# Attention's second exponential written to SBUF, with two shared buffers in place of three

## The chip, the cores and the metric

The kernel runs on one core of one Trainium2 chip. The metric is device time in microseconds (us), lower is better. A core has five engines that matter here: TensorE (PE; its weight loads are listed apart as PEld), VectorE (DVE), ScalarE (ACT), GpSimd (POOL) and SyncE (SP, which issues most DMAs). Each works through its own instructions in order and waits for the others by semaphores. PSUM is the memory that PE writes; SBUF holds everything else on the chip.

## The reference

One layer of an encoder on 1024 prompt tokens and 64 tokens of a running stream. One input projection feeds eight heads of forgetting attention and four heads of a gated recurrence (HGRN2); both are gated and meet in an output projection. The change touches the attention of the prompt alone:

```python
def fox_attend(q, k, v, c_q, c_k, q_pos, k_pos):
    s = jnp.einsum('bqhd,bkhd->bhqk', q.astype(F32), k.astype(F32)) * (FOX_HEAD_DIM ** -0.5)
    s = s + (jnp.swapaxes(c_q, 1, 2)[..., :, None] - jnp.swapaxes(c_k, 1, 2)[..., None, :])
    mask = k_pos[None, :] <= q_pos[:, None]
    s = jnp.where(mask, s, -jnp.inf)
    p = jax.nn.softmax(s, axis=-1)
    return jnp.einsum('bhqk,bkhd->bqhd', p.astype(v.dtype), v)
```

`q` and `k` have 8 heads of 64 columns; `c` is the running sum of the log forget values.

## The kernel before

**Precision.** Matmuls run on a rounded float type (`F32R`). To keep float32 accuracy a value is split into a high part, rounded to `F32R`, and a low part, the rest; products of high with high, high with low and low with high are added up. For the attention weights the high part `ph` is the exponential of the scores written as `F32R` (L848). The exponential is then computed a second time in float32 (L849), and DVE subtracts `ph` from it to get the low part `pl` (L850).

**Stages.** A first part projects the values (to about 80 us). Then comes attention, in which PE also runs the projections of queries, keys and others as filler (L248, L229; `Filler` and `merge` hand them out by cost). Then the recurrence with the remaining projections, and at last the output projection.

**Attention.** The heads go in the order of `PAIRS`, two heads `s` to a pair `p_`. Each head has two chunks `c` of 512 queries, with 4 and 8 blocks `b` of 128 keys. The last four blocks of a chunk cross the diagonal and have 512, 384, 256 and 128 query columns. `scores` (L834) makes a block: two matmuls into a PSUM bank `st` (L842 and L843), the mask added by DVE on the diagonal (L845), the two exponentials on ACT, the subtraction on DVE. `values` (L856) multiplies with the values two blocks later (`LAG = 2`): three matmuls of line L867, with `ph`, `pl` and again `ph`, into a bank `av`. At the end of a chunk L873 to L875 divide by the row sums through a tile of the tag `tmp`. The sample's exponentials (`pt`, L898 to L900) and one step of the projection `hi` (L238) use the same tag.

**Buffers.** `st` has two banks (`PSB`), so a block's L842 needs that the block two before it has been read out. `ph` and `pl` have three buffers each (`PB`), `tmp` has three (`TMPB`).

**Work beside it.** While a head runs, `prepare` readies the next: ACT copies high parts (L717, L737, L748), POOL subtracts low parts (L722, L738, L754), PE and DVE find row maxima (L795, L797, L801, L812 to L814), DVE makes two columns of them (L760, L761) and SP brings them into rows of `QY` by small DMAs (L780). `QY` is read by L843 and L896. Weights come by DMA into one raw buffer (L163); ACT makes the high part in four pieces (L174), POOL the low part (L175), and the next load starts after the last piece.

**Order.** The order in which the generators hand out the work is the program's. A list scheduler then places each engine's instructions, so that a change of what a tile waits for also moves neighbours.

Of the kernel before, what the change touches and what calls it, by code (L numbers as in the profile page):

```python
# [8 lines left out]
F32 = mybir.dt.float32  # L9
F32R = mybir.dt.float32r  # L10
U8 = mybir.dt.uint8
AF = mybir.ActivationFunctionType
ALU = mybir.AluOpType
AX = mybir.AxisListType

P = 128
# [10 lines left out]
EPS = 1e-6  # L27
NEG = -3.0e38

WBUFS, PB, TMPB, NBUF, OGB, GB = 4, 3, 3, 8, 3, 7  # L30
PSB = dict(pj=2, tp=2, st=2, av=2)


# [30 lines left out]
def f32(ap):  # L64
    return ap.bitcast(F32)
# [3 lines left out]
def tile_fox_hgrn2(  # L69
# [7 lines left out]
    act, dve, pool, pe, sync = nc.scalar, nc.vector, nc.gpsimd, nc.tensor, nc.sync  # L77
# [7 lines left out]
    def nm(s):  # L85
        cnt[0] += 1
        return f"{s}_{cnt[0]}"
# [4 lines left out]
    def bank(tag):  # L92
        return ps.tile([P, 512], F32, tag=tag, name=nm(tag), bufs=PSB[tag])
# [561 lines left out]
    with actx:  # L655
        ap = actx.enter_context(tc.tile_pool(name="att", bufs=1, reuse_waits="tile"))
        a2 = actx.enter_context(tc.tile_pool(name="att2", bufs=2, reuse_waits="tile"))
# [176 lines left out]
        def scores(p_, s, c, b):  # L834

            kx, ky, qx, qy = KX[s], KY[s], QX[s], QY[s]
            q0 = max(0, b - 4 * c) * P
            n = 512 - q0
            ks = slice(b * P, (b + 1) * P)
            qs = slice(c * 512 + q0, (c + 1) * 512)  # L840
            st = bank("st")
            pe.matmul(st[:, :n], kx[:, ks], qx[:, qs], start=True, stop=False)  # L842
            pe.matmul(st[:, :n], ky[YM[s], ks], qy[YM[s], qs], start=False, stop=True)  # L843
            if b >= 4 * c:
                dve.tensor_tensor(st[:, :P], st[:, :P], kmask[:], op=ALU.add)  # L845
            ph = a2.tile([P, 512], F32R, tag="ph", name=nm("ph"), bufs=PB)
            pl = a2.tile([P, 512], F32R, tag="pl", name=nm("pl"), bufs=PB)
            act.activation(ph[:, :n], st[:, :n], AF.Exp)  # L848
            act.activation(st[:, :n], st[:, :n], AF.Exp)  # L849
            dve.tensor_tensor(pl[:, :n], st[:, :n], f32(ph[:, :n]), op=ALU.subtract)  # L850
            queue.append((p_, s, c, b, ph, pl))
            return 2 * n / 2.4

# [24 lines left out]
        def chunk_main(p_, s, c):  # L878
            for b in range(4 * (c + 1)):
                yield scores(p_, s, c, b)  # L880
                yield values() if len(queue) > LAG else 0.0
# [615 lines left out]
    for i, rows, src in tok_tiles[:SAMPLE_POS] + tok_tiles[NT:] + tok_tiles[SAMPLE_POS:NT]:  # L1497
# [11 lines left out]
        st = fin.tile([P, 1], F32, tag="sst", name=nm("sst"), bufs=3)  # L1509
# [94 lines left out]
```

## Time and profile before

| what | value |
|---|---|
| median of 3 runs | 689.65 us (689.0 to 690.16) |
| the profiled execution | 689.64 us, span 687.9 us |
| mean granted TensorE clock | 0.999 |
| share of PE, DVE, ACT, POOL in the span | 98%, 61%, 47%, 22% |
| L849 (second exponential), 96 times | 46.6 us on ACT |
| L850 (subtraction), 96 times | 53.0 us on DVE |
| L867 (three groups), 96 times each | 33.4, 33.0 and 32.4 us on PE |

The span goes from the first to the last instruction. A group's row in the profile reads: line, engine, operation, tiles written and read, shape, how often; then busy us and mean ns of one; then the idle time of the engine before them and what ended it. A row of a timeline begins with the start and the length in us; idle time before it, with what ended it, stands in brackets. A row of the waits reads: who waited for whom, us in total, times, longest. Matmuls overlap, and their ends are modelled, so that their lengths are longer than the spacing of their starts.

### The profile page before, as it was taken

To read this page: it belongs to the slowest core of one execution; us is meant where nothing else is said; L and a number is where in the kernel's file an instruction comes from. 1 tells how busy PE (TensorE), PEld (TensorE's weight loads), DVE (VectorE), ACT (ScalarE), POOL (GpSimd) and SP (SyncE) were. 2 spreads that over 40 slices of the span, in tenths; PEclk is the share of its full clock that TensorE was granted. 3 is DMA by queue.
4 is the path that set the end of the run, shared out by engine and by line. 5 is a ranking of instruction groups with operands and counts; after the bars stand their busy time and mean duration, and the time that the engine had idled before them with its cause. 6 is when DMAs were issued, how large, how long until landed. Compare 5 with 4: busy or idle time off the path is not lost.

```text
span 687.9 us, 13216 instructions
## 1 busy us (share of the span) xinstructions
PE 674.5 (98%) x4952; PEld 608.4 (88%) x4952; DVE 423.0 (61%) x1058; ACT 325.2 (47%) x826; POOL 152.2 (22%) x217
## 2 busy tenths in 40 slices
PE   9999999999999999899999999999999999999996
PEld 7888998898889899689999999999999998878885
DVE  4536267776666774775687365563965679754541
ACT  6845644746465664656443423432423344414532
POOL 4045832523343323301000100010000100103422
PEclk9999999999999999999999999999999999999999
DMA  8923312222222311211311110121111115421211
GB/s 314 338 84 112 109 40 80 65 61 45 65 55 52 71 26 40 80 12 32 116 43 32 43 33 31 32 71 35 32 40 54 40 37 184 126 83 61 93 47 61
DMA packets 40715, 51.17 MB, mean 74 GB/s; under 512 B 22870, under 2 KB 25766, under 8 KB 40652
## 3 DMA queue, kind: packets, MB, share of 16 engines
q1 hardware_dynamic: 40476, 50.25, 24.6%
q8 instruction: 39, 0.64, 0.4%
q14 instruction: 24, 0.20, 0.1%
q10 hardware_dynamic: 176, 0.09, 0.1%
HBM read 36.32 MB, written 9.56 MB: 67 GB/s over the span
## 4 chain that ended last, share of the span: by engine, by line
PE 67%; DVE 1%; DMA 1%; SPq 1%; POOL 1%; ACT 1%; issue 0%; POOLq 0%; DVEq 0%; ACTq 0%
PE pj L248 30%; PE pj L1383 13%; PE pj L229 7%; PE av L867 4%; PE st L842 2%; PE st L1114 1%; PE st L843 1%; PE st L1274 1%; PE pj L1377 1%; PE tp L795 1%; SPq L780 1%; DMA wr<-in_w_t_dram 1%; PE tp L1301 1%; PE av L1301 1%; PE tp L1303 1%; PE tp L1255 1%
## 5 line engine op out<-in xcount | busy, mean ns | idle before, releaser
L248 PE MATMUL pj<-hT,whi 128*128 128x364 f32 (+1 forms) x1152 | 218.8, 330 | 0.0
L248 PEld LDWEIGHTS pj<-hT,whi 128*128 128x128 f32 x1152 | 194.2, 188 | 6.6 <-issue 0.3
L248 PE MATMUL pj<-hT,wlo 128*128 128x364 f32 (+1 forms) x576 | 115.6, 332 | 0.0
L248 PEld LDWEIGHTS pj<-hT,wlo 128*128 128x128 f32 x576 | 96.9, 188 | 3.1 <-issue 0.2
L848 ACT ACTIVATE ph<-st 128x512 fp32r<-128x512 f32 (+1 forms) x96 | 46.8, 488 | 65.3 <-DVE st L845 42.7
L850 DVE TENSOR_TENSOR pl<-st,ph 128x512 fp32r<-128x512 f32 (+1 forms) x96 | 53.0, 553 | 30.7 <-ACT st L849 30.1
L109 POOL TENSOR_SCALAR rr<-ss 128x4 f32<-128x4 f32 (+1 forms) x12 | 2.3, 190 | 257.2 <-ACT og L1307 256.9
L1383 PE MATMUL pj<-hT,mx 128*128 128x512 f32 (+1 forms) x264 | 56.3, 374 | 0.0
L1383 PEld LDWEIGHTS pj<-hT,mx 128*128 128x128 f32 x264 | 46.2, 188 | 10.0
L175 POOL TENSOR_TENSOR wlo<-wr,whi 128x256 fp32r<-128x256 f32 (+1 forms) x52 | 36.8, 736 | 75.6 <-ACT ph L848 39.7
L174 ACT ACTIVATE whi<-wr 128x256 fp32r<-128x256 f32 (+1 forms) x112 | 38.1, 406 | 29.5 <-PE pj L248 18.1
L849 ACT ACTIVATE st<-st 128x512 f32<-128x512 f32 (+1 forms) x96 | 46.6, 485 | 0.0
L842 PE MATMUL st<-QX,KX 128*128 128x512 f32 (+1 forms) x96 | 34.9, 364 | 2.7 <-DVE pl L850 2.2
L229 PE MATMUL pj<-whi,hT 128*128 128x264 f32 (+1 forms) x256 | 36.2, 284 | 0.1
L1383 PE MATMUL pj<-hT,mxp 128*128 128x512 f32 x144 | 36.0, 402 | 0.0
L867 PE MATMUL av<-ph,VH 128*128 128x512 f32 (+1 forms) x96 | 33.4, 348 | 1.8 <-ACT ph L848 1.8
L229 PEld LDWEIGHTS pj<-whi,hT 128*128 128x128 f32 x256 | 33.6, 188 | 1.4 <-DVE q L1067 0.3
L843 PE MATMUL st<-QY,KY 68*128 68x512 f32 (+3 forms) x96 | 33.4, 348 | 0.4 <-DMA QY<-mxs 0.4
L867 PE MATMUL av<-pl,VH 128*128 128x512 f32 (+1 forms) x96 | 33.0, 344 | 0.0
L867 PE MATMUL av<-ph,VL 128*64 128x512 f32 (+1 forms) x96 | 32.4, 337 | 0.0
L795 PE MATMUL tp<-KY,QY 66*128 66x128 f32 (+5 forms) x96 | 32.2, 352 | 0.0
L1383 PEld LDWEIGHTS pj<-hT,mxp 128*128 128x128 f32 x144 | 26.4, 188 | 6.3 <-ACT mxp L1370 0.3
(295 smaller groups left out, 1202.6 us busy)
## 6 DMA issues: line engine op xcount, KB each, us to landing
wr<-in_w_t_dram SPq DMA_DIRECT2D x24, 512.0 KB
x<-in_xT_dram SPq DMA_DIRECT2D x16, 272.0 KB
xn<-in_x_prompt_dram SPq DMA_DIRECT2D x8, 512.0 KB
wo_raw<-in_w_out_dram SPq DMA_DIRECT2D x8, 512.0 KB
yp<-in_x_prompt_dram SPq DMA_DIRECT2D x6, 512.0 KB
out_dram<-yp SPq DMA_DIRECT2D x12, 256.0 KB
out_dram<-kT SPq DMA_DIRECT2D x4, 544.0 KB
wv<-in_w_v_dram SPq DMA_DIRECT2D x8, 256.0 KB
```

The costliest lines, as they stand in the source:

```text
L174: act.activation(hf[:, cs], raw[:, cs], AF.Copy)
L175: self.eng.tensor_tensor(lf[:, cs], raw[:, cs], f32(hf[:, cs]), op=ALU.subtract)
L229: pe.matmul(pb[:rows, :width], a[:, j, t0:t0 + rows], w[j // 4][b][:, j % 4, :], start=(g == 0 and j == 0), stop=(g == 2 and j == 7))
L248: pe.matmul(pb[:, :n], w[:, j, :], h[:, j, t0:t0 + n], start=(g == 0 and j == 0), stop=(g == 2 and j == 7))
L795: pe.matmul(pb[:, :n], qy[rows, qs], ky[rows, k0:k0 + n], start=True, stop=True)
L842: pe.matmul(st[:, :n], kx[:, ks], qx[:, qs], start=True, stop=False)
L843: pe.matmul(st[:, :n], ky[YM[s], ks], qy[YM[s], qs], start=False, stop=True)
L848: act.activation(ph[:, :n], st[:, :n], AF.Exp)
L849: act.activation(st[:, :n], st[:, :n], AF.Exp)
L850: dve.tensor_tensor(pl[:, :n], st[:, :n], f32(ph[:, :n]), op=ALU.subtract)
L867: pe.matmul(av[mm, cols], w[:, b, :], x[:, :n], start=(b == 0 and w is VH[s] and x is ph), stop=(b == nblk - 1 and w is VL[s]), skip_group ...
L1383: pe.matmul(pb[:rows, :n], mx[:, a, j, :rows], wo[b][:, j0 + j, c0:c0 + n], start=(g == 0 and j == 0), stop=(g == 2 and j == nj - 1))
```

## The change

The second exponential goes to a new SBUF tile `pe` of its own (tag `pe`, one buffer, 512 columns) and no longer over the scores in PSUM. The subtraction reads `pe` and `ph`, both in SBUF. The tag `tmp` has two buffers of 512 columns in place of three. Lines after L848 stand one further down in the changed kernel: L850 is the second exponential, L851 the subtraction, L868 the value matmuls, L874 to L876 the division.

```diff
-WBUFS, PB, TMPB, NBUF, OGB, GB = 4, 3, 3, 8, 3, 7
+WBUFS, PB, TMPB, NBUF, OGB, GB = 4, 3, 2, 8, 3, 7
...
             act.activation(ph[:, :n], st[:, :n], AF.Exp)
-            act.activation(st[:, :n], st[:, :n], AF.Exp)
-            dve.tensor_tensor(pl[:, :n], st[:, :n], f32(ph[:, :n]), op=ALU.subtract)
+            ps_ = a2.tile([P, 512], F32, tag="pe", name=nm("pe"), bufs=1)
+            act.activation(ps_[:, :n], st[:, :n], AF.Exp)
+            dve.tensor_tensor(pl[:, :n], ps_[:, :n], f32(ph[:, :n]), op=ALU.subtract)
```

The scheduler's order moves in places. On ScalarE at the start of the third head (156.9 to 160.8 us of the profile before), the rows before; `QY` and `VH` are parts for the next head, `rd` the division of the chunk before, `ph` and `st` the blocks of this head:

```order
L748 ACTIVATE QY_543<-qT_1145 64x576
L737 ACTIVATE VH_545<-vnat_93 128x8x64
L873 ACTIVATE rd_1795<-av_1572 64x512
L848 ACTIVATE ph_1784<-st_1780 128x384
L849 ACTIVATE st_1780<-st_1780 128x384
L874 ACTIVATE rd_1795<-rd_1795 64x512
L848 ACTIVATE ph_1811<-st_1807 128x256
L849 ACTIVATE st_1807<-st_1807 128x256
```

The same place in the changed kernel:

```order
L748 ACTIVATE QY_543<-qT_1151 64x576
L737 ACTIVATE VH_545<-vnat_93 128x8x64
L848 ACTIVATE ph_1809<-st_1805 128x384
L850 ACTIVATE pe_1812<-st_1805 128x384
L874 ACTIVATE rd_1821<-av_1591 64x512
L848 ACTIVATE ph_1837<-st_1833 128x256
L875 ACTIVATE rd_1821<-rd_1821 64x512
L850 ACTIVATE pe_1840<-st_1833 128x256
```

The logarithm of the division (L873, now L874) has moved behind both exponentials of the block of 384 columns, and the other half of the division between those of the next block.

On PE at the seventh head, at the end of its first chunk (288 to 291 us of the profile before), the rows before; `pj` is a projection, `tp` the row maxima (L795) or the sample's scores (L895), `st_3374` the first block of the second chunk:

```order
L895 MATMUL tp_3425<-QX_681,KX_679 128x64
L867 MATMUL av_3351<-ph_3344,VH_544 128x256
L248 MATMUL pj_3453<-hT,whi_3183 128x364 x2
L795 MATMUL tp_3473<-KY_541,QY_543 128x512
L248 MATMUL pj_3521<-hT,whi_3183 128x364 x5
L842 MATMUL st_3374<-QX_681,KX_679 128x512
L843 MATMUL st_3374<-QY_542,KY_540 128x512
```

The same place in the changed kernel:

```order
L868 MATMUL av_3426<-ph_3418,VH_544 128x256
L248 MATMUL pj_3532<-hT,whi_3250 128x364
L842 MATMUL st_3450<-QX_681,KX_679 128x512
L896 MATMUL tp_3503<-QX_681,KX_679 128x64
L248 MATMUL pj_3532<-hT,whi_3250 128x364 x3
L843 MATMUL st_3450<-QY_542,KY_540 128x512
```

L842 of the block has moved ahead of the projection matmuls, four of them stand in front of its L843 where seven stood, and the row maximum L795 comes after it.

## The prediction

> **What bounds the kernel now.** I read the profile from the outside in: the busy line of the page, then the busy time of three stretches (before, during and after attention), then the list of who waited for whom, then the instructions around one wait.
>
> ```profile
> PE 674.5 (98%) x4952; PEld 608.4 (88%) x4952; DVE 423.0 (61%) x1058; ACT 325.2 (47%) x826; POOL 152.2 (22%) x217
> 0.00:80.00 80.00, 78.33 (x382) 67.48 (x383) 35.99 (x76) 47.26 (x93) 34.31 (x69) 1.00 0.57 199
> 80.00:333.00 253.00, 247.89 (x1500) 221.68 (x1499) 167.54 (x464) 144.78 (x335) 83.15 (x87) 1.00 0.23 53
> 333.00:688.00 355.00, 348.28 (x3074) 319.27 (x3072) 219.51 (x518) 133.12 (x400) 34.73 (x62) 1.00 0.20 62
> ```
>
> PE is the bound everywhere; its granted clock is 1.00 in all three stretches. The change lies in the second one, attention, from 80 to 333 us. The columns after the length are PE, PEld, DVE, ACT and POOL. PE is idle there for 253.00 - 247.89 = 5.1 us. Nothing in the change shortens a matmul, so about 5 us is all that it can win. DVE is busy for 66% of this stretch, ACT for 57%, POOL for 33%.
>
> ```profile
> PEld st L842 <- DVE pl L850: 6.6, 15, 1.0
> PE st L842 <- DVE pl L850: 2.2, 6, 0.7
> PE av L867 <- ACT ph L848: 1.8, 3, 1.1
> PE st L843 <- DMA QY<-mxs: 0.4, 1, 0.4
> PE tp L896 <- DMA QY<-mxs: 0.3, 1, 0.3
> ```
>
> These rows give total us, how often, and the longest. The first two are one wait, seen from the weight load and from the matmul: the first score matmul of a block (L842) wants an `st` bank, and the subtraction L850 two blocks back has not yet read it out. It is the largest cause of idle PE time here. Here is the worst case, in order of time:
>
> ```profile
> 157.59 0.63 ACT L737 ACTIVATE VH<-vnat 128x512 fp32r<-128x512 f32 x1
> 158.24 0.59 ACT L873 ACTIVATE rd<-av 64x512 f32<-64x512 f32 x1
> 158.86 0.49 ACT L848 ACTIVATE ph<-st 128x384 fp32r<-128x384 f32 x1
> 159.14 1.27 POOL L738 TENSOR_TENSOR VL<-vnat,VH 128x512 fp32r<-128x512 f32 x1
> 159.25 0.49 ACT L849 ACTIVATE st<-st 128x384 f32<-128x384 f32 x1
> 159.77 0.56 DVE L850 TENSOR_TENSOR pl<-st,ph 128x384 fp32r<-128x384 f32 x1 [1.29 <-ACT st L849]
> 160.36 0.68 DVE L875 TENSOR_TENSOR mixF<-av,rd 64x512 f32<-64x512 f32 x1
> 160.38 0.33 PE L842 MATMUL st<-QX,KX 128*128 128x128 f32 x1 [0.73 <-DVE pl L850]
> 161.39 0.33 PE L867 MATMUL av<-pl,VH 128*128 128x384 f32 x1
> ```
>
> The bank passes through both exponentials and the subtraction, and L842 starts 0.05 us after L850 ends at 160.33.
>
> **The change part by part.** *1. The bank is let go by the second exponential.* It ends at 159.25 + 0.49 = 159.74, 0.59 us before the subtraction. The new ScalarE order also puts the first exponential ahead of L873 here, which is another 0.59 us. Together that is 1.18 us against a wait of 0.73 us, so this wait goes. What is late next is the `pl` matmul (last row), which sits 161.39 - 160.33 = 1.06 us behind the subtraction.
>
> ```profile
> L248 PEld LDWEIGHTS pj<-hT,whi 128*128 128x128 f32 x1152 | 194.2, 188 | 6.6 <-issue 0.3
> ```
>
> How much do the 15 waits hold in all? At least the 2.2 us of the matmul row. At most, each of them also exposes a weight load, 188 ns in this group of the page: 2.2 + 15 x 0.188 = 5.0 us. I take the middle, **-3.6 us**.
>
> *2. Durations.* They hardly change:
>
> ```profile
> L848 ACT ACTIVATE ph<-st 128x512 fp32r<-128x512 f32 x48 | 28.6, 595 | 28.5 <-PE st L843 12.9 <-DVE st L845 12.3 <-DVE mxs L761 2.3
> L849 ACT ACTIVATE st<-st 128x512 f32<-128x512 f32 x48 | 28.4, 591 | 0.0
> L850 DVE TENSOR_TENSOR pl<-st,ph 128x512 fp32r<-128x512 f32 x48 | 33.0, 687 | 17.9 <-ACT st L849 17.7
> L1362 DVE TENSOR_TENSOR hT<-wo_raw,hT 128x512 fp32r<-128x512 f32 x16 | 10.3, 681 | 0.0
> ```
>
> L848 already writes SBUF and takes 595 ns, where L849 takes 591 ns into PSUM. L1362 is the same subtraction with both inputs in SBUF, 681 ns against 687 ns. A few ns on engines that are 57% and 66% busy: 0.
>
> *3. The subtraction now has two inputs in SBUF while POOL works.* The next rows give minimum, median and maximum of a line in ns, then one case, then the subtraction's busy time in the stretch:
>
> ```profile
> L850 DVE TENSOR_TENSOR pl<-st,ph x96: 271/614/694, 91.5 to 331.0; 128x512 fp32r<-128x512 f32 x48, 128x384 fp32r<-128x384 f32 x16, 128x256 fp32r<-128x256 f32 x16, 128x128 fp32r<-128x128 f32 x16
> L761 DVE SCALAR_TENSOR_TENSOR mxs<-mx,mxs x24: 143/158/693, 86.3 to 307.1; 128x4 fp32r<-128x4 f32 x16, 64x1 fp32r<-64x1 f32 x8
> 216.32 1.35 POOL L722 TENSOR_TENSOR KX<-kT,KX 64x544 fp32r<-64x544 f32 x1 [7.47 <-ACT KX L717]
> 217.10 0.59 DVE L761 SCALAR_TENSOR_TENSOR mxs<-mx,mxs 64x1 fp32r<-64x1 f32 x1
> 80.00:333.00 253.00, 53.04 (x96) 1.00 0.23 53
> ```
>
> L761 reads two SBUF tiles. It is over a few elements and mostly takes 158 ns, but at 217.10 it took 0.59 us and ended at 217.69, 0.02 us after POOL's subtraction ended at 217.67. Today's L850, with one input in PSUM, never took over 694 ns. So I expect the changed subtraction to be held whenever it starts inside a POOL subtraction.
>
> The size: POOL is busy 83.15 of 253 us, so 33% of 96 subtractions, 32, start inside one of its 87 instructions of 83.15 / 87 = 0.96 us mean, and wait half of one: 32 x 0.48 = 15 us of DVE time. Whether POOL is held by DVE in turn no row shows; if so, 53.04 / 253 = 21% of its 87, 18, wait half of a 0.55 us subtraction: 5 us. The Trainium skill, in "SBUF — State Buffer", section "Who interferes with whom", speaks against this change: a VectorE instruction with two SBUF inputs contends with a GpSimd one that reads SBUF, and whichever issues second blocks fully until the first is done. The L761 row agrees as far as DVE goes; by this rule POOL's 5 us come on top, as in the slow rival below.
>
> Behind a held subtraction on DVE stand the masks L845, for which first exponentials wait, the row maxima (L797, L801), which hold `tp` banks, and the evacuations of `pj`. But neither engine is the bound, and the bank no longer waits for DVE, so most of these 20 us stay beside PE. One place where they reach it is clear:
>
> ```profile
> 272.33 1.42 POOL L175 TENSOR_TENSOR wlo<-wr,whi 128x256 fp32r<-128x256 f32 x2
> 272.41 0.69 DVE L850 TENSOR_TENSOR pl<-st,ph 128x512 fp32r<-128x512 f32 x1
> 273.78 0.33 SPq L163 DMA_DIRECT2D wr<-in_w_t_dram  x1
> 277.62 1.33 ACT L174 ACTIVATE whi<-wr 128x256 fp32r<-128x256 f32 x4 [1.96 <-DMA wr<-in_w_t_dram]
> 279.38 0.44 PE L867 MATMUL av<-ph,VH 128*128 128x384 f32 x1 [1.12 <-ACT ph L848]
> ```
>
> The subtraction starts inside the first of two POOL pieces. The load of the next weights (L163) waits for the second, ScalarE waits for that load, and the first exponential behind it is what PE waits for at 279.38. Slip the subtraction between the two pieces and this wait grows by up to one subtraction, 0.7 us. Elsewhere a held subtraction can make its `pl` matmul late, as in the case at 161.39, where 1.06 us of slack are mostly used up by the gain of part 1. I add 0.5 us for all such. Bounds of this part: 0 and 20 us; taken, by the nearest row, **+1.2 us**.
>
> *4. The scheduler moves scores ahead of projection matmuls.* POOL and SP keep their order; some 60 matmuls of PE move. In the piece shown above, L842 and L843 of a block move ahead of projection matmuls, where L843 waits for the rows that DMA brings (0.4 us today, then L896 0.3 us). From the last L795 in front of the L812 of this head to this L843, 22 projection matmuls stood in the order and 15 stand now, and one L795 moves behind.
>
> ```profile
> 192.46 0.67 PE pj L248 x4
> ```
>
> At 0.67 / 4 = 0.17 us, seven of them are 1.2 us less cover in front of that DMA, and the matmuls come later. The other way, the same moves let first exponentials run earlier there. Bounds: -0.5 (the waits there go) and +1.4; taken **+1.0 us**.
>
> *5. One SBUF buffer for the second exponential.* It waits for the subtraction of the block before:
>
> ```profile
> 127.73 0.69 DVE L850 TENSOR_TENSOR pl<-st,ph 128x512 fp32r<-128x512 f32 x1 [0.79 <-ACT st L849]
> 127.99 0.49 ACT L849 ACTIVATE st<-st 128x384 f32<-128x384 f32 x1
> 130.16 0.38 ACT L848 ACTIVATE ph<-st 128x256 fp32r<-128x256 f32 x1
> ```
>
> Here it would be held from 127.99 to 128.42, 0.43 us. Behind it on ScalarE stand L873, L737, L874 and the next first exponential at 130.16, for which PE's L867 waits. But blocks come every 253 / 96 = 2.6 us and a subtraction takes 0.55 us, so this happens only where short blocks crowd. Bounds: 0, and such a hold in each of the 16 chunks, all of it on PE's path, 16 x 0.43 = 6.9 us. The next first exponential here is 1.7 us away, so nearly all hides; taken **+0.3 us**.
>
> *6. Two `tmp` buffers in place of three.* A `tmp` tile lives from L873 to the end of the multiplication L875, in the case above 161.04 - 158.24 = 2.8 us, and 25 are used in 253 us (two for the chunks and one for the sample of each of 8 heads, one for `hi`), one every 10 us. The second-last is always free: 0. If that cover went, L873 would be late, and behind it a first exponential, as in part 5.
>
> The sum against the profiled execution (689.64 us, of which 687.9 us is the span, 1.7 us around it): -3.6 + 1.2 + 1.0 + 0.3 = -1.1, so 688.5 us. The median of the runs shown is 689.65 us, the same.
>
> **The rivals.** *All of the gain arrives.* PE idles only where the bank is late, the held subtractions hide, and the moved scores help ScalarE as much as they cost: -3.6 us and a little of part 4, 686.0 us. For it: 15 waits of one cause. Against it: 0.7 us of rows at 272 us and the DMA at L843.
>
> *The subtraction held by POOL decides, and it is slower.* The place is the start of each head, where POOL's L754 and L738 (1.3 to 1.4 us each) fall among four short blocks, and the weights at 272 us. It turns the sign once more than 3.6 - 1.3 = 2.3 us of the 20 reach PE. At a quarter, 5 us, the time is 689.6 - 2.3 + 5 = 692.3 us. For it: DVE is the busiest helper and its masks (L845) stand behind the held subtraction. Against it: the bank no longer depends on DVE, and the other waits of PE for DVE's results are not among its largest.
>
> *It does nothing.* The bank comes earlier, but PE waits at the next thing, `pl` or the first exponential, for just as long: 689.6 us.
>
> **How the numbers follow.** A difference of under 0.2%, 1.4 us, can hardly be told from none. Forecast 688.5 us (own range 687.4 to 689.6) 42%; full gain 28%; held by POOL 20%; nothing 10%. The forecast lies near the line of 0.2%, at 688.3 us: a quarter of it, 10%, is beyond. Faster 28 + 10 = 38%, same 32 + 10 = 42%, slower 20%. The range from 686.0 to 691.8 leaves out half of the full gain's spread below and half of the slow case.
>
> **What would show it.** Right: the waits of L842 for DVE are gone, L842 waiting for ACT stays under 1 us; subtractions inside POOL instructions take up to 1.4 us more than now, DVE's busy time in attention grows by 10 to 15 us; the wait for `ph` at the weights after the `hi` projection grows by some 0.7 us and that of L843 for DMA by 1 us. Wrong: subtractions still end below 0.7 us (no hold), `pl` appears as PE's largest wait (held by POOL), or the idle time of PE in attention falls to 2 us (full gain).

## The result and the profile after

| what | before | after |
|---|---|---|
| median | 689.33 us (688.53 to 690.16, 4 runs) | 694.53 us (694.09 to 695.13, 4 runs) |
| the profiled execution | 689.64 us, span 687.9 us | 694.09 us, span 692.3 us |
| mean granted TensorE clock | 0.999 | 0.995 |

The changed kernel is slower by 5.2 us: 1.0077 times the time before, with an interval from 1.0064 to 1.009. That lies outside the predicted range.

First the busy line of the page after, the row of attention (PE, PEld, DVE, ACT, POOL, then the clock), and the changed subtraction's row (minimum, median and maximum in ns):

```profile
PE 676.9 (98%) x4952; PEld 609.6 (88%) x4952; DVE 434.2 (63%) x1058; ACT 325.5 (47%) x826; POOL 157.4 (23%) x217
80.00:333.00 253.00, 245.89 (x1471) 218.59 (x1470) 177.45 (x461) 143.78 (x332) 86.00 (x83) 0.99 0.22 51
L851 DVE TENSOR_TENSOR pl<-pe,ph x96: 271/682/3039, 91.4 to 335.3; 128x512 fp32r<-128x512 f32 x48, 128x384 fp32r<-128x384 f32 x16, 128x256 fp32r<-128x256 f32 x16, 128x128 fp32r<-128x128 f32 x16
```

The span grew by 4.4 us. PE's busy time grew by 676.9 - 674.5 = 2.4 us of them, with the same 4952 matmuls, so its matmuls ran slower; the other 2.0 us are more idle time. DVE is busy for 9.9 us more in attention and POOL for 2.9 us more. One subtraction took 3.04 us. Next, who waited for whom on PE after:

```profile
PE tp L896 <- DVE mx L797: 2.8, 1, 2.8
PE av L868 <- ACT ph L848: 1.2, 1, 1.2
...
PE tp L795 <- DMA QY<-KY: 1.0, 2, 0.8
PE tp L812 <- DVE mx L797: 0.5, 1, 0.5
PE st L842 <- ACT pe L850: 0.5, 2, 0.3
PE av L868 <- DVE pl L851: 0.5, 2, 0.2
```

The waits of L842 for DVE are gone, as they should be, and 0.5 us of waiting for ACT is left. But a single wait of 2.8 us, which the profile before does not have, stands at the top. These rows of the timeline after show its place, the first block of the second chunk of the fifth head (two expectations below call it the seventh):

```profile
226.18 1.30 POOL L754 TENSOR_TENSOR QX<-qT,QY 64x512 fp32r<-64x512 f32 x1 [0.74 <-ACT QY L748]
...
227.09 3.04 DVE L851 TENSOR_TENSOR pl<-pe,ph 128x512 fp32r<-128x512 f32 x1 [0.42 <-ACT pe L850]
...
227.45 3.28 POOL L175 TENSOR_TENSOR wlo<-wr,whi 128x264 fp32r<-128x264 f32 x4
227.52 0.40 PE L843 MATMUL st<-QY,KY 68*128 68x512 f32 x1
230.05 0.55 DVE L797 CUSTOM_DVE_ANT_0 tp<-tp,cmask 128x384 f32<-128x384 f32 x1
230.16 0.60 ACT L850 ACTIVATE pe<-st 128x512 f32<-128x512 f32 x1 [2.62 <-DVE pl L851]
...
230.72 0.30 PE L896 MATMUL tp<-QX,KX 128*128 128x64 f32 x1 [2.80 <-DVE mx L797]
```

The subtraction starts inside L754, which ends at 226.18 + 1.30 = 227.48 us. There it was to get in, by the prediction. It was held on through three of the four pieces L175, and ended only at 227.09 + 3.04 = 230.13 us, inside the fourth, which ends at 230.73 us and was held in turn. This is the fourth alone; each of the first three took 0.73 us:

```profile
229.54 1.18 POOL L175 TENSOR_TENSOR wlo<-wr,whi 128x264 fp32r<-128x264 f32 x1
```

So the subtraction missed its turn at three ends, that of L754 and those of two pieces, and got in at the fourth. The row maximum L797 stands behind the subtraction on DVE, and holds the `tp` bank that PE's L896 needs. ScalarE waits too, for the one buffer `pe`. The windows from 226 us on show what followed on PE (PE's busy time comes second, the granted clock third from the right):

```profile
226.00:228.00 2.00, 1.92 (x12) 1.34 (x10) 1.58 (x6) 1.54 (x4) 1.82 (x2) 1.00 0.35 75
228.00:230.00 2.00, 0.00 (x0) 0.00 (x0) 2.00 (x1) 0.00 (x0) 2.00 (x4) 1.00 0.00 1
230.00:232.00 2.00, 1.28 (x9) 1.15 (x10) 2.00 (x9) 1.79 (x4) 0.73 (x1) 0.98 0.19 39
232.00:234.00 2.00, 2.00 (x7) 1.54 (x6) 1.53 (x5) 1.97 (x6) 0.00 (x0) 0.50 0.67 224
234.00:236.00 2.00, 2.00 (x12) 1.71 (x10) 1.39 (x2) 0.67 (x2) 0.73 (x1) 0.66 0.15 5
```

PE did nothing for 2 us. About a microsecond after it started again its clock was halved, for 3.4 us. What that takes away is 2 x (0.02 + 0.50 + 0.34) = 1.72 us of full clock. The stall and the clock are 2.8 + 1.7 = 4.5 us at one place, nearly the whole loss. The attention of the kernel before has no such dip.

It is not the only hold. Of the 96 subtractions some 25 others took longer than the same width does in the kernel before, by 9 us in all. One of them, in the fourth head, missed a turn as well; a subtraction of 384 columns took 0.56 us before:

```profile
190.13 1.43 POOL L754 TENSOR_TENSOR QX<-qT,QY 64x576 fp32r<-64x576 f32 x1 [2.82 <-PE st L843]
...
191.36 1.86 DVE L851 TENSOR_TENSOR pl<-pe,ph 128x384 fp32r<-128x384 f32 x1 [0.74 <-ACT pe L850]
...
191.51 1.29 POOL L738 TENSOR_TENSOR VL<-vnat,VH 128x512 fp32r<-128x512 f32 x1
```

It meets L754 0.2 us before its end, and comes in only at the end of L738. PE itself does not wait behind it.

### The profile page after: what moved, and what is told of

Its sections match the earlier page's. It is cut to its first block, busy times and chain, and to the rows that moved or that the text cites. A ratio compares the mean times of both kernels' runs of the same rounds, so it can differ in the third digit from the quotient of the medians.

```text
span 692.3 us, 13132 instructions
## 1 busy us (share of the span) xinstructions
PE 676.9 (98%) x4952; PEld 609.6 (88%) x4952; DVE 434.2 (63%) x1058; ACT 325.5 (47%) x826; POOL 157.4 (23%) x217
## 4 chain that ended last, share of the span: by engine, by line
PE 90%; DVE 4%; ACT 3%; DMA 1%; issue 1%; SPq 1%; DVEq 0%; POOLq 0%; POOL 0%; ACTq 0%
PE pj L248 40%; PE pj L1384 13%; PE pj L229 7%; PE av L868 6%; PE tp L795 2%; PE st L842 2%; PE st L843 2%; PE pj L462 2%; PE st L462 2%; PE av L462 2%; PE tp L462 2%; PE st L1115 1%; PE st L1275 1%; DVE pl L851 1%; PE pj L1378 1%; PE pj L221 1%
## 5 line engine op out<-in xcount | busy, mean ns | idle before, releaser
L851 DVE TENSOR_TENSOR pl<-pe,ph 128x512 fp32r<-128x512 f32 (+1 forms) x96 | 64.5, 672 | 28.3 <-ACT pe L850 27.1
L848 ACT ACTIVATE ph<-st 128x512 fp32r<-128x512 f32 (+1 forms) x96 | 46.9, 489 | 63.0 <-DVE st L845 51.4
L175 POOL TENSOR_TENSOR wlo<-wr,whi 128x256 fp32r<-128x256 f32 (+1 forms) x52 | 40.3, 804 | 74.9 <-ACT whi L174 39.3
L850 ACT ACTIVATE pe<-st 128x512 f32<-128x512 f32 (+1 forms) x96 | 46.6, 485 | 5.1 <-DVE pl L851 4.8
L842 PE MATMUL st<-QX,KX 128*128 128x512 f32 (+1 forms) x96 | 34.7, 361 | 0.5 <-ACT pe L850 0.5
L868 PE MATMUL av<-ph,VH 128*128 128x512 f32 (+1 forms) x96 | 33.7, 351 | 1.3 <-ACT ph L848 1.2
L868 PE MATMUL av<-pl,VH 128*128 128x512 f32 (+1 forms) x96 | 34.1, 355 | 0.7 <-DVE pl L851 0.5
L843 PE MATMUL st<-QY,KY 68*128 68x512 f32 (+3 forms) x96 | 34.0, 355 | 0.2 <-DMA QY<-mxs 0.2
L795 PE MATMUL tp<-KY,QY 66*128 66x128 f32 (+5 forms) x96 | 32.6, 356 | 1.0 <-DMA QY<-KY 1.0
L868 PE MATMUL av<-ph,VL 128*64 128x512 f32 (+1 forms) x96 | 32.7, 341 | 0.0
```

Source lines behind the costliest of these rows:

```text
L175: self.eng.tensor_tensor(lf[:, cs], raw[:, cs], f32(hf[:, cs]), op=ALU.subtract)
L795: pe.matmul(pb[:, :n], qy[rows, qs], ky[rows, k0:k0 + n], start=True, stop=True)
L850: act.activation(ps_[:, :n], st[:, :n], AF.Exp)
L851: dve.tensor_tensor(pl[:, :n], ps_[:, :n], f32(ph[:, :n]), op=ALU.subtract)
L868: pe.matmul(av[mm, cols], w[:, b, :], x[:, :n], start=(b == 0 and w is VH[s] and x is ph), stop=(b == nblk - 1 and w is VL[s]), skip_group ...
```

## The experiments

The theory after this reading: **one long hold, and the clock behind it, make the loss**. Rivals: one of the buffers, many small holds, or the changed order. A second question was where the predicted gain of 3.6 us had gone.

**The buffers.** The kernel before with `tmp` in two buffers, and the changed kernel with two buffers for `pe` (room for the second came from a `tmp` with one):

```diff
-WBUFS, PB, TMPB, NBUF, OGB, GB = 4, 3, 3, 8, 3, 7
+WBUFS, PB, TMPB, NBUF, OGB, GB = 4, 3, 2, 8, 3, 7
```

> The kernel before with two tmp buffers in place of three, nothing else. The theory (a DVE subtraction with both inputs in SBUF is held by POOL) and the rival of the single exponential buffer both expect no difference, 689.3 us within 0.7. If the third tmp buffer had been needed, part of the 5.2 us shows here.

```diff
-WBUFS, PB, TMPB, NBUF, OGB, GB = 4, 3, 2, 8, 3, 7
+WBUFS, PB, TMPB, NBUF, OGB, GB = 4, 3, 1, 8, 3, 7
...
-            ps_ = a2.tile([P, 512], F32, tag="pe", name=nm("pe"), bufs=1)
+            ps_ = a2.tile([P, 512], F32, tag="pe", name=nm("pe"), bufs=2)
```

> The changed kernel with two buffers for the second exponential, paid for by leaving one tmp buffer. The hold theory expects 692 to 695 us: DVE is held just as long at 227 us, and PE waits there for a tp bank that DVE frees, not for ScalarE; a subtraction of over 2.5 us remains. The rival (ScalarE waits for the one buffer) expects 688 to 690 us. One tmp buffer may cost up to 1 us of its own by either.

The first took 689.61 us, ratio 1.000 [0.999, 1.001]: the third `tmp` buffer is worth nothing. The second took 696.94 us, 1.011 [1.0095, 1.0125]. The hold of 3.04 us and the stall of 2.8 us are there as before, so the single `pe` buffer doesn't make them. A `tmp` with one buffer may cost something of its own; the two were not tried apart. In this trace L868 waits 3.2 us for the first exponential at 281 us, and the clock is halved for 6.8 us at 230 us and for 3.4 us at 285 us.

**Less on POOL at that place.** The pieces L175 at 227 us belong to the weights of `hi`. In the changed kernel and in the kernel before, DVE makes these eight pieces:

```diff
-                self.eng.tensor_tensor(lf[:, cs], raw[:, cs], f32(hf[:, cs]), op=ALU.subtract)
+                (dve if c0 == C_HI else self.eng).tensor_tensor(lf[:, cs], raw[:, cs], f32(hf[:, cs]), op=ALU.subtract)
```

> The changed kernel, but the eight low parts of the weights of the first hi projection (128x264, L175) go to DVE in place of POOL; nothing else. The hold theory expects the stall of 2.8 us at 227 us and the time at half clock behind it to go: 689.5 to 691 us. The rivals (single buffer, scheduler's order) have no reason for a gain: 694 to 695 us.

> The kernel before with the same eight low parts on DVE: the control for the run above. The hold theory expects no gain, 689.3 us within 0.7, since no subtraction of before is ever held.

692.77 us, 1.0052 [1.0036, 1.0069], and the control 690.28 us, 1.001 [1.0001, 1.002]. The difference between the two shrank from 5.2 to 2.5 us, and the stall at L896 to 0.7 us. That is less than I expected: another stall took its turn, this row of the waits of the changed one:

```profile
PE av L868 <- ACT ph L848: 1.5, 1, 1.5
```

It ends at 280 us, and the clock is 0.50 again from 283 us on. This is the wait for the weights that the prediction had picked, and a subtraction is indeed held between two pieces L175 there, at 273 us. In the kernel before and in the control the wait is 1.1 us long, in the changed kernel 1.2, and the clock stays at 1.00 behind it. So this edit takes back half of the loss, and a second stall with the clock behind it takes the first one's place.

**No hold at all.** All of POOL's subtractions in attention (L175, L722, L738, L754) are replaced by two fills each, which read nothing; the low parts of the weights, keys, values and queries that POOL makes are left out. One of the four:

```diff
-            pool.tensor_tensor(VL[s][:], vn, f32(VH[s][:, :, 0:HD]), op=ALU.subtract)
+            for _ in range(2):
+                pool.memset(f32(VL[s][:]), 0.0)
```

> The changed kernel with each low part that POOL makes during attention (L175, L722, L738, L754) replaced by two memsets of the same tile, so that POOL still works there but reads no SBUF; this leaves out the low parts of keys, queries, values and of the weights split on POOL. The hold theory expects no subtraction (L851) over 0.72 us, no wait of PE for DVE over 0.5 us, and 2 to 4 us less than the same edit of the kernel before: 685 to 688 us. If the scheduler's order or the single buffer made the loss, it stays above the control by 2 us or more.

> The kernel before with the same memsets, leaving out the same low parts: the control. POOL is not what PE waits for in it, so 688 to 690 us by every theory, with the waits of L842 for L850 still there.

The changed kernel took 686.35 us, 0.9951 [0.9929, 0.9972], the control 685.95 us, 0.9949 [0.9933, 0.9966]. The control was expected no faster than 688 us: POOL's own subtractions cost both kernels 3 us, which I hadn't seen; why is not shown, for the fills are also shorter (two of 0.31 us for a piece of 128x264) and wait for no high part. What counts here is that the two are alike. Of the changed one, the subtraction's row and the two largest of PE's waits in attention:

```profile
L858 DVE TENSOR_TENSOR pl<-pe,ph x96: 273/591/694, 91.5 to 326.8; 128x512 fp32r<-128x512 f32 x48, 128x384 fp32r<-128x384 f32 x16, 128x256 fp32r<-128x256 f32 x16, 128x128 fp32r<-128x128 f32 x16
```

```profile
PE tp L802 <- DMA QY<-KY: 1.5, 2, 0.9
...
PE st L849 <- ACT pe L857: 0.6, 2, 0.3
```

No subtraction is over 694 ns, although 18 of them started inside a fill, so the hold comes from POOL's reading subtractions and from nothing else here. Without it the change costs nothing, and wins nothing either: PE comes earlier to the row maxima (L802, L795 in the changed kernel) and waits there for the DMA L746, which stands behind the row DMAs L780 on SP.

**The subtraction on POOL.**

```diff
-            dve.tensor_tensor(pl[:, :n], ps_[:, :n], f32(ph[:, :n]), op=ALU.subtract)
+            pool.tensor_tensor(pl[:, :n], ps_[:, :n], f32(ph[:, :n]), op=ALU.subtract)
```

> The changed kernel with the subtraction itself on POOL. DVE loses 53 us of work and is never held by it; POOL gets 96 subtractions of some 0.4 to 1.3 us, about 95 us more. If the hold alone is what costs, 686 to 690 us, unless POOL's queue becomes late: then the pl matmul waits for POOL, and 692 to 700 us. The single-buffer rival expects more waits of ScalarE than in the changed kernel, since the buffer is read later.

703.0 us, 1.0191 [1.0167, 1.0215]. It is no way out. POOL takes up to 1.30 us for it, and `pl` is late:

```profile
PE av L868 <- POOL pl L851: 9.3, 10, 2.3
```

**Which chunk.** Of the 2.2 us that PE waits in L842 before, all but 0.3 us lies in first chunks; the long hold lies in a second one. The new form in the first chunk of each head only, and in the second only (`c == 1`):

```diff
-            ps_ = a2.tile([P, 512], F32, tag="pe", name=nm("pe"), bufs=1)
+            ps_ = a2.tile([P, 512], F32, tag="pe", name=nm("pe"), bufs=1) if c == 0 else st
```

> The changed kernel with the new form in the first chunk of each head only (blocks 0 to 3); in the second chunk the exponential goes over the scores in PSUM as before. All but 0.75 us of the 4.65 us that L842 started late before lies in blocks 1 to 3, which wait for blocks of the first chunk (and for the last of the chunk before), so the bank's gain should stay nearly whole: 2 to 2.8 us less at L842. Theory (the 3.04 us hold at 227 us, in the first block of a second chunk, and the clock after it make the loss): that hold cannot occur, and the time is 688 to 690 us. Rival (many small holds and the changed order make the loss): 691.5 to 693 us.

> The complement: the new form in the second chunk of each head only (blocks 4 to 11), the old form in the first. Little gain at L842 (under 0.8 us). Theory (one long hold with the clock behind it): if the subtraction of the block at 227 us meets the same GpSimd instructions, 692 to 694 us; if the order shifts it past them, 689 to 690.5 us, and the trace shows no stall over 2 us. Rival (small holds in the first chunk and the order): 689 to 690.5 us although a stall over 2 us is there.

690.08 us, 1.0012 [1.0001, 1.0024], and 695.45 us, 1.0085 [1.0072, 1.0098]. The loss goes with the second chunk, as the theory has it. In the second kernel a hold of 3.02 us stalls L896 for 2.3 us, and the clock is halved from 233 to 240 us. The first kernel's runs fall apart: four with a mean clock of 0.997 or more take 688.16 to 688.76 us, eight with 0.993 to 0.995 take 689.4 to 691.65 us. The profiled one is of the second kind; its windows, columns as above:

```profile
288.00:290.00 2.00, 0.83 (x5) 0.69 (x5) 2.00 (x5) 0.47 (x2) 0.70 (x1) 1.00 0.08 1
290.00:292.00 2.00, 1.58 (x13) 1.38 (x12) 1.34 (x6) 1.98 (x5) 0.00 (x0) 0.78 0.65 143
292.00:294.00 2.00, 2.00 (x6) 1.41 (x6) 1.47 (x4) 1.94 (x6) 0.00 (x0) 0.50 0.08 1
294.00:296.00 2.00, 2.00 (x6) 1.51 (x5) 0.91 (x2) 1.48 (x4) 0.00 (x0) 0.50 0.12 1
296.00:298.00 2.00, 2.00 (x9) 1.18 (x7) 1.97 (x4) 0.14 (x1) 0.00 (x0) 0.52 0.12 1
```

Here 1.6 us without matmuls in four were enough, and 2 x (0.22 + 0.50 + 0.50 + 0.48) = 3.4 us of clock went, twice the loss of the changed kernel.

**The DMA behind the row DMAs.** L746 is issued on ScalarE's queue, past the row DMAs on SP; in the kernel before as a control, and with the new form in first chunks:

```diff
-                sync.dma_start(f32(QY[s][2:4, :]), f32(KY[s][4:6, 0:T]))
+                act.dma_start(f32(QY[s][2:4, :]), f32(KY[s][4:6, 0:T]))
```

> The kernel before with the DMA of L746 (the key-side rows copied into QY) issued on ScalarE's queue, no longer behind the row DMAs L780 on SP. Before, L795 waits little for it (0.32 us in three places), so 688.8 to 690 us. It is the control for the same move in the changed kernel, where L795 starts 1.8 us late in total; if the issue on ScalarE costs 0.6 us eight times on the path of the first exponentials, up to 692 us.

> The new form in the first chunks only, and the DMA of L746 on ScalarE's queue. In a_c0 L795 starts 1.6 us late in all, most of it on this DMA, and L843 waits 1.2 us for row DMAs. If that DMA behind the row DMAs on SP is what eats the bank's gain: 688 to 689.2 us, faster than before. If the wait only passes to the next thing: 689.3 to 690.5 us.

> The same kernel as a_c0_qact. If the early release is worth about 1 us where no hold and no late DMA take it back: a ratio of 0.997 to 0.9995 again. If the first measurement was chance: an interval around 1.

The control took 689.73 us, 1.0006 [0.9996, 1.0016]. With the new form in first chunks it is 688.33 us, 0.9988 [0.9978, 0.9997], and again 688.39 us, 0.9986 [0.9971, 1.0]. In its list of waits L795 no longer stands. Of the versions that compute the same, this is the one that beats both kernels, the one before by 1.0 us; that is close to the noise, and the second interval reaches 1. What the moved DMA does is not settled by it. The four runs of the first-chunk form with a high clock (688.16 to 688.76 us) are as fast without the move. Of the 22 runs with it none has a mean clock below 0.997, where the first-chunk form alone has 8 of 12. So the move may pay by keeping the clock up, more than by L795's wait itself. Either way the early release of the bank is worth about 1 us, when neither a long stall nor a halved clock stands in its way.

**Why the subtraction misses its turn.** A test ahead of the kernel before ran POOL's subtractions back to back beside ten of DVE's for each kind; the loop over the kinds is left out here. Three rows with two SBUF inputs, and two where the first input lies in PSUM:

```diff
...
+            for j in jobs:
+                sub(j)
+            for w in widths:
+                pin(dve.tensor_copy(sa[:, :w], sa[:, :w]))
+                pin(dve.tensor_tensor(dc[:], src[:], db[:], op=ALU.subtract))
```

> The kernel before with a test ahead of it: GpSimd runs subtractions back to back (64x576 x10, 128x512 x10, 128x256 x18, and 64x576 followed by four of 128x256, three times), while VectorE runs ten 128x512 subtractions with copies inside PSUM of different widths between them. Theory: with two SBUF inputs each subtraction is held to the end of the GpSimd instruction it meets and gets in before the next one: at most 0.69 + 1.4 = 2.1 us beside 64x576 and 128x512, 0.69 + 0.75 = 1.45 us beside 128x256. Rival (it misses its turn when another GpSimd instruction is ready): some over 2.1 us, with two or more GpSimd instructions inside. With one input in PSUM: 0.69 us throughout. GpSimd is held in turn by up to 0.7 us where VectorE is inside.

```profile
72.31 9.34 POOL L113 TENSOR_TENSOR mbp<-mbp,mbp 64x576 f32<-64x576 f32 x7 [0.18 <-DVE st L124]
...
73.11 1.61 DVE L125 TENSOR_TENSOR mbd<-mbd,mbd 128x512 f32<-128x512 f32 x1
...
79.35 1.73 DVE L125 TENSOR_TENSOR mbd<-mbd,mbd 128x512 f32<-128x512 f32 x1
...
90.71 8.48 POOL L113 TENSOR_TENSOR mbp<-mbp,mbp 64x576 f32<-64x576 f32 x9 [0.38 <-DVE st L124]
91.45 0.68 DVE L125 TENSOR_TENSOR mbd<-st,mbd 128x512 f32<-128x512 f32 x1
```

With PSUM every subtraction took 0.68 us. With two SBUF inputs all 36 that met a POOL instruction were held to its end, and got in before the next: 1.88 us was the longest. POOL was held in turn: its 128x256 piece took 1.05 us in place of 0.72. But these POOL instructions wait for each other, with gaps of 0.08 us; in the kernel the next one starts some 0.03 us before the last has ended. Two more tests were to tell whether that decides:

> The kernel before with a second test ahead of it: short chains of GpSimd subtractions (six of 128x256; three of 128x512; 64x576 and four of 128x256; 64x576 and 128x512), each met by one VectorE subtraction with two SBUF inputs at a different point. In most chains each GpSimd instruction writes a tile of its own and waits for nothing; in two kinds they write the same tile and so wait for each other. Theory (a turn is passed only in a gap between two GpSimd instructions): in the chains without waits some subtractions pass one or more ends of GpSimd instructions, with holds over 1.45 us beside 128x256 and over 2.1 us in the others; in the chains with waits none. Rival (the turn is passed at the end of each instruction; the long hold has another cause): none over these bounds anywhere.

> The kernel before with a third test ahead of it, 18 chains: GpSimd 64x512 and four of 128x256 (six times), 64x512 and 128x512 (six times), each instruction writing a place of its own; and six times the first kind with each instruction overlapping the one before by 8 columns, so that it waits for it. One ScalarE instruction starts both engines; VectorE's subtraction with two SBUF inputs comes 0.2 to 1.2 us later. Theory (a turn is passed only in a gap between two GpSimd instructions): in the first two kinds some subtractions are held past an end (over 2.1 us in all, two or more GpSimd instructions inside), in the third kind none. Rival: in no kind.

They hardly did: in 34 of the 36 chains of the first the subtraction came ahead of POOL's first instruction, and the second had a gap of 0.08 us behind every instruction that a subtraction met. Neither has a hold past one end. In the two chains that are left the next POOL instruction starts 0.03 to 0.04 us before the end, and the subtraction gets in at that end all the same.

The changed kernel's own trace says more. Eight subtractions were held there by an L175 with the next POOL instruction 0.04 to 0.05 us ahead of its end, and all eight got in at that end. The two that missed a turn had met L754. So a start without a gap is not enough; L754 in front was part of it each time.

Next, in the kernel itself, a small copy behind L754 (with its control), and then pieces L175 that overlap by 8 columns and so wait for each other:

```diff
...
             pool.tensor_tensor(QX[s][r, cs], qT[r, cs], f32(QY[s][r, cs]), op=ALU.subtract)
+            pool.tensor_copy(gapt[r, 0:8], f32(QX[s][r, cs.stop - 8:cs.stop]))
```

> The changed kernel with a small GpSimd copy (64x8) behind each L754 that reads its result and so waits for it to end. Theory (the missed turn behind L754 makes the long stall): the subtraction at the seventh head gets in right behind L754, held by about 0.4 us, no stall of L896 over 1 us, no drop of the clock there, 689.5 to 691.5 us. Rival (the turn is missed for another reason): a hold over 2 us and the 2.8 us stall remain, 693.5 to 695.5 us.

> Control: the kernel before with the same copies. Both theories: 689 to 690 us, since GpSimd is busy for a third of attention and 16 copies of 0.1 to 0.2 us hide.

```diff
             for z in range(W_PIECES):
...
+                cs = slice(cs.start - 8 * (z > 0 and self.eng is pool), cs.stop)
                 self.eng.tensor_tensor(lf[:, cs], raw[:, cs], f32(hf[:, cs]), op=ALU.subtract)
```

> The changed kernel, with each of GpSimd's pieces of the weights from the second on starting 8 columns earlier, over columns that the piece before has written (the same values again), so that it must wait for that piece to end. Theory (a turn is passed only in a gap): the subtraction at the seventh head gets in behind the first piece, held by about 1.2 us in place of 2.3 us; L896 waits 1.6 us or less, the clock falls less or not, 691.5 to 693.5 us. Rival (the turn is missed gap or no gap): held by 2.3 us again, 694 to 695.5 us.

The copy took 696.57 us, 1.0101 [1.0084, 1.0118], the control 689.28 us, 0.9996 [0.9985, 1.0007]. It missed its mark: the scheduler put the four pieces between L754 and the copy, so that the hold met the same five instructions and lasted 3.03 us; the clock was halved for 6.8 us behind it, twice as long as in the changed kernel. The overlapping pieces took 692.62 us, 1.0049 [1.0032, 1.0066], as the theory expected. Their rows at the same place, one line further down:

```profile
227.43 1.29 POOL L755 TENSOR_TENSOR QX<-qT,QY 64x512 fp32r<-64x512 f32 x1 [0.77 <-ACT QY L749]
...
228.35 0.93 DVE L852 TENSOR_TENSOR pl<-pe,ph 128x512 fp32r<-128x512 f32 x1 [0.44 <-ACT pe L851]
...
228.68 3.22 POOL L176 TENSOR_TENSOR wlo<-wr,whi 128x264 fp32r<-128x264 f32 x3
```

```profile
PE tp L897 <- DVE mx L798: 0.8, 1, 0.8
```

The subtraction arrives 0.92 us into the same instruction as before (0.91), and is let in at its end. The stall is 0.8 us and the clock stays at 1.00. PE, ScalarE and DVE have the same instructions in the same order in both kernels, so getting the turn back is worth about 694.53 - 692.62 = 1.9 us. That is less than the 2.0 + 1.7 = 3.7 us by which stall and clock fell at this place; the rest turned up as other waits. L176 follows here as closely as in the changed kernel, so what stands further behind on POOL seems to count. Yet the other miss, at 191 us with L738 alone behind L754, is there in this kernel too (1.87 us). What in POOL's queue decides it stays open. The remaining 3.3 us over the kernel before are spread: L868 waits 1.8 us at one place, L844 0.9 us for row DMAs and L796 0.8 us for L746.

**What is left of the theory.** The holds make the loss: without them the two kernels differ by 0.4 us, with them by 5.2, so they are worth some 4.8 us. The one long hold with its clock is 1.9 us of that by the overlapping pieces, and 5.2 - 2.5 = 2.7 us by the pieces on DVE. The rest, 2 to 3 us, goes with the other holds, so for that the rival of many small holds is right. That the changed order adds nothing is shown only as far as the fills go, which bring an order of their own.

## Why the prediction was wrong

**The failed step is the size of part 3** ("wait half of one", "most of these 20 us stay beside PE", +1.2 us). The sum of the holds was about right: I put 15 us on DVE and 5 us on POOL, and DVE's busy time in attention grew by 9.9 us, POOL's by 2.9 us. What I took for granted was that a hold ends with the POOL instruction it meets, so at most 1.4 us. One hold lasted through three ends to a fourth and took 2.3 us more than the subtraction needs, another through one end to a second and took 1.3 us more. The first reached PE by a way that I had named among the things behind it, the row maxima that hold `tp` banks, and judged to be covered. And I gave an idle PE no price beyond its idle time: the halved clock added 1.7 us. The place that I had picked, the weights at 272 us, stayed as it was in the changed kernel (1.2 us after, 1.1 us before), and grew to 1.5 us with the pieces on DVE.

By the pair without holds this term measures 5.2 - 0.4 = 4.8 us in place of 1.2, and all the others together 0.4 us in place of -2.3. These two errors, 3.6 and 2.7 us, make up the whole of the miss, from -1.1 to +5.2 us. The pair changes POOL's work too, so the split is an estimate.

**Part 1** (-3.6 us) was right in its mechanism and mis-sized. The waits of L842 for DVE went, but the pair without holds shows 686.35 against 685.95 us, so nothing of it arrived; the version with L746 moved shows 1.0 us. I added up lateness at one matmul and did not ask which transfer the earlier PE would then run into. The third rival said just that, though of `pl` and the first exponential and not of a DMA.

**Part 2** (durations: 0) held: with no hold the subtraction's maximum is 694 ns, as before. **Part 4** (+1.0 us at L843) did not come: L843's wait for the row DMAs fell from 0.4 to 0.2 us, while L795 got one of 1.0 us for L746. The sign of the queue's effect was right, the DMA was another. **Part 5** (+0.3 us): ScalarE was held by the one buffer 7 times, 4.8 us in all, more than I thought, but the second buffer did not help. **Part 6** (0) is confirmed by the kernel before with two.

The rival "the subtraction held by POOL decides" (692.3 us) had the right engines and the right POOL instruction, L754, though it looked for it at the start of a head and not of a second chunk; it too lacked the long hold and the clock. By the Trainium skill, in "SBUF — State Buffer", section "Who interferes with whom", whichever of the two issues second blocks until the first is done. The test agrees for both sides (36 of 36, and 1.05 against 0.72 us). The 3.04 us show that the end of the first is no bound: the next ones can take the turn.

## What to carry to other kernels

Before a DVE subtraction's second input moves from PSUM to SBUF, look at the longest unbroken row of POOL instructions it can meet, not at their mean, and at what stands behind it on DVE; most holds here ended at the first end, but two did not. A freed bank is worth only what the next thing in line allows: look for the transfer that an earlier PE runs into, and try the new form only where the waits are. Where PE is the bound, a stall of some 2 us can cost the clock behind it as well, so one such place can outweigh a dozen removed waits of 0.3 us.

## What was not expected of the hardware

The granted clock fell to 0.50 after 2.8 us without matmuls in the changed kernel, and after 1.6 us of idle time within four in the kernel with the new form in first chunks, whose mean clock was low in 8 of 12 runs. In the traces of these kernels all seven stalls of 2.2 us and more in attention cost it; one of 1.8 us (the overlapping pieces) did not, and of two of 1.5 us one did. What it takes comes in equal parts: 1.7 us in the changed kernel, 3.4 us (twice that) in the two kernels with one chunk only. The Trainium skill, in "TensorE: Matmul & The Clock Gate", section "Part 1: The HAM clock gate", has the clock gated to half after an idle window of some 3.4 us that runs freely. Half a clock over 3.4 us is 1.7 us, which agrees with these parts, and a free window would explain that the same stall costs the clock in some runs only; but in attention no PE was idle for a whole 3.4 us (the longest stall is 3.2 us), so a shorter idle time was enough.

A DVE instruction with two SBUF inputs was let in at the end of the POOL instruction it met in all 36 cases of the test, and missed up to three ends in the kernel, at the same place in four kernels (3.02 to 3.04 us). At a second place, in the fourth head, a subtraction of 384 columns missed one end in all seven kernels that have the new form in first chunks, with the subtraction on DVE and POOL's reads as they are (1.78 to 1.88 us in place of 0.56).
